# One head's K in four loads, the merge's gates two chunks ahead, and the output weights' splits shared out anew

## The chip, the cores and the metric

The kernel runs on one core of a Trainium2 chip. The metric is the device time of one execution in microseconds (us). The engines are named as in the profile: PE (TensorE, matrix multiplications), DVE (VectorE), ACT (ScalarE), POOL (GpSimd) and SP (SyncE, which here issues every DMA, in program order).

## The reference

One layer of a diffusion backbone, for 1024 latent tokens and 128 context tokens, D = 1024, 8 heads in each of two branches:

```python
h = layernorm(x) * (1 + scale) + shift            # adaLN, scale/shift/gate from the condition
qa, ka, va, za, qr, kr, vr, zr = split(h @ w_in)
oa = (softmax(q1 k1^T / 8) - lam * softmax(q2 k2^T / 8)) @ v   # keys: cached context + latent tokens
oa = (rmsnorm(oa) * subln_g * (1 - lam_init) * silu(za)) @ w_pa
orr = retention(qr, kr, vr, forward) + retention(backward)     # chunkwise recurrence
orr = (layernorm(orr) * ret_gn_g * silu(zr)) @ w_pr
ga, gr = split(sigmoid(h @ w_gate + b_gate))
m = ga * oa + gr * orr
y = layernorm(2**0.25 * x + gate * (m @ w_out)) * ln_g + ln_b
```

Context tokens read only context; latent tokens read both. Outputs are y and the context's keys, values and retention states.

## The kernel before, in words

All 1152 tokens (1024 latent, 128 context) are held as columns. Every float32 operand of a matmul is split into a high part and a low part of the type float32r, and each product is three matmuls (high by high, high by low, low by high). `hi_of` makes a high part on ACT, `lo_of` the low part on DVE ("v") or POOL ("p").

A dense job (`Job`) multiplies one block of 128 output columns' weights with all tokens, in NC = 3 chunks of CW = 384 tokens, 24 matmuls a chunk, into a PSUM bank called `dn`, of which there are two. Its `pre(c)` runs ahead of a chunk, its `evac(c, ps)` empties the bank. `dense` loads and splits the weights one job ahead (tiles `raw`, `whi`, `wlo`).

The whole program is emitted in one order. A small planner (`Sched`) keeps a modelled time for PE, ACT, DVE and POOL, lets several Python generators take turns at it, and so fixes the order of the instructions on every engine. `sch.later` puts off a piece of work to a modelled time; `sch.guard(tag, bufs)` makes such pieces run at once, so that a buffer can be taken again. DMAs cost the planner nothing: they go into SP's queue at the place where they are called, and SP runs them in that order, each waiting for its buffer and its data.

The stages, by the time in the profile:

- up to about 580 us: adaLN, projections, retention (`phase_h`, `phase_a`). Each head's rotated K is stored as high and low parts in `Kd`, 2 x 1280 columns for each of 128 partitions.
- about 590 to 1316 us: attention (`phase_b`). `softmax_stream` goes through `seq`, 8 heads h of 5 steps c; a step is two tiles of 128 queries (c = 4 one tile, the context's). At the start of a step it asks for the next step's Q (`load_q`, four DMAs), at c = 1 for the next head's K (`load_k`). Scores go to the one PSUM buffer `S`; DVE takes the maximum `nm`, ACT the exponentials `E`. `pv_stream` transposes E, splits it and multiplies with V (`load_v`). Between these matmuls the planner puts dense jobs: gates (`g_job`), the retention branch's silu gate (`zr_job`), the attention branch's (`z_job`). These two end in `gate_out`, which uses the tiles `tz`, `goh`, `gol` (two buffers each) and stores `goh` and `gol` to `ORd` or `OAd`. The gates go to `Gd` as tanh(u/2).
- about 1380 to 1486 us, the first merge pass: 8 jobs `pr_job(j)` multiply the retention branch (tiles `X`, two of them in K's buffers) with `w_pr`. The evacuation multiplies by the gate, read back from `Gd` into a tile `gt`, and stores the product in `Td`. `merge_in(kind, j, c)` issues the gate's load: for a chunk's successor, at the end of its evacuation. Meanwhile the attention branch comes back from `OAd` into `Y`, and `ada_gate` computes the adaLN gate on DVE.
- about 1486 to 1590 us, the second: `pa_job(j)` does the same for the attention branch, adds the product read back from `Td` into a `tz` tile, and writes the sum's high and low parts to `X`. In its last job the weights `w_out` arrive in eight pieces (`w_out_load(n)`) and the first four are split (`w_out_split(n)`) into the place of `Y`; the other four are split right after it. Pieces 0 to 3 hold the left half of the output columns, two row blocks each; 4 to 7 the right half.
- to the end: `out_stream`, the output product (PSUM tile `e`, 24 matmuls of 512 columns for a part) and the last LayerNorm. Its parts begin with the left halves of tiles 0 and 1, then their right halves.

## Time and profile before

| | |
|---|---|
| median of 3 runs | 1690.24 us (1687.55 to 1691.09) |
| the profiled execution | 1692.03 us, of which the span from first to last instruction is 1690.2 |
| granted TensorE clock, mean | 0.994 |
| PE busy | 1657.3 us, 98% of the span, 10515 matmuls |
| DVE, ACT, POOL busy | 853.6, 606.1, 784.4 us |
| DMA | 237.36 MB, mean 140 GB/s |

In a row of grouped or single instructions stand the start and the length in us, the engine, the line of the kernel, the operation, the tile written and the tiles read, the shape, and in brackets how long the engine stood idle before and what ended that. Many operations go through helpers, so that line 149 is every matmul, 156 every ACT operation, 164 and 173 DVE's, 185 and 189 POOL's, 203 every DMA: the tiles' names tell them apart. A row of stretches has the window, its length, then for PE, PEld, DVE, ACT and POOL the busy time with the number of instructions, then the granted clock, the DMA engines' busy share and GB/s. A row of the chain has start, length and what the chain ran through. A matmul's length in these rows overlaps the next one's, so paces are read from start to start.

### The profile page before, as it was taken

To read this page: it belongs to the slowest core of one execution; us is meant where nothing else is said; L and a number is where in the kernel's file an instruction comes from. 1 tells how busy PE (TensorE), PEld (TensorE's weight loads), DVE (VectorE), ACT (ScalarE), POOL (GpSimd) and SP (SyncE) were. 2 spreads that over 40 slices of the span, in tenths; PEclk is the share of its full clock that TensorE was granted. 3 is DMA by queue.
4 is the path that set the end of the run, shared out by engine and by line. 5 is a ranking of instruction groups with operands and counts; after the bars stand their busy time and mean duration, and the time that the engine had idled before them with its cause. 6 is when DMAs were issued, how large, how long until landed. Compare 5 with 4: busy or idle time off the path is not lost.

```text
span 1690.2 us, 27057 instructions
## 1 busy us (share of the span) xinstructions
PE 1657.3 (98%) x10515; PEld 1610.2 (95%) x10515; DVE 853.6 (51%) x1679; ACT 606.1 (36%) x1136; POOL 784.4 (46%) x546
## 2 busy tenths in 40 slices
PE   7999999999999999999999999999999999999998
PEld 4799999999999999999999999999999999999886
DVE  7736407314605536656565666566656033134666
ACT  5532222221221245455455555545555220012200
POOL 2246227334725657654757475757655321112200
PEclk9999999999999999999999999999999999999999
DMA  8254303421321383534434343525252577854532
GB/s 332 94 149 127 123 27 114 128 93 45 104 102 44 125 267 111 189 106 133 139 116 146 113 155 110 162 92 168 74 160 87 208 263 262 264 180 131 159 125 87
DMA packets 135697, 237.36 MB, mean 140 GB/s; under 512 B 15801, under 2 KB 103313, under 8 KB 134545
## 3 DMA queue, kind: packets, MB, share of 16 engines
q1 hardware_dynamic: 135568, 235.63, 43.3%
q8 instruction: 83, 1.36, 0.3%
q14 instruction: 46, 0.37, 0.1%
HBM read 161.08 MB, written 74.49 MB: 139 GB/s over the span
## 4 chain that ended last, share of the span: by engine, by line
PE 89%; DVE 3%; issue 2%; ACT 2%; DMA 1%; POOL 1%; SPq 0%; DVEq 0%; POOLq 0%; ACTq 0%
PE dn L149 59%; PE S L149 8%; PE o L149 6%; PE e L149 6%; PE a L149 5%; PE tp L153 5%; PE tp L149 1%; ACT E L156 1%; DMA xt<-in_x 1%; DMA ORd<-goh 0%; DVE eps L173 0%; DVE r L173 0%; DVE E L173 0%; ACT whi L156 0%; DVE nm L1097 0%
## 5 line engine op out<-in xcount | busy, mean ns | idle before, releaser
L149 PE MATMUL dn<-Y,whi 128*128 128x384 f32 x3200 | 829.7, 340 | 3.3 <-DVE rt L164 2.2
L149 PEld LDWEIGHTS dn<-Y,whi 128*128 128x128 f32 x3200 | 567.4, 189 | 4.9 <-DVE rt L164 2.5
L149 PE MATMUL dn<-Y,wlo 128*128 128x384 f32 x1600 | 535.6, 336 | 0.0
L185 POOL TENSOR_TENSOR wlo<-raw,whi 128x1024 fp32r<-128x1024 f32 x85 | 204.7, 2412 | 412.5 <-ACT whi L156 403.1
L149 PEld LDWEIGHTS dn<-Y,wlo 128*128 128x128 f32 x1600 | 300.5, 188 | 1.4 <-issue 0.9
L1097 DVE TENSOR_REDUCE nm<-S 128x1 f32<-128x1152 f32 x144 | 178.1, 1237 | 174.2 <-PE S L149 173.9
L189 POOL TENSOR_SCALAR E<-E,r 128x640 f32<-128x640 f32 x64 | 143.6, 2243 | 127.5 <-DVE r L173 87.0
L156 ACT ACTIVATE E<-S,nm 128x1152 f32<-128x1152 f32 x144 | 162.3, 1127 | 79.4 <-DVE nm L1097 74.5
L149 PE MATMUL dn<-whi,Y 128*128 128x256 f32 x864 | 158.9, 284 | 2.4 <-ACT vr L156 1.9
L149 PEld LDWEIGHTS dn<-whi,Y 128*128 128x128 f32 x864 | 135.4, 191 | 2.8 <-ACT vr L156 2.1
L149 PE MATMUL o<-wTh,V 128*128 128x256 f32 x576 | 133.5, 290 | 0.0
L156 ACT ACTIVATE wTh<-tp 128x512 fp32r<-128x512 f32 (+1 forms) x168 | 88.6, 543 | 112.9 <-PE tp L153 109.2
L156 ACT ACTIVATE whi<-raw 128x1024 fp32r<-128x1024 f32 x88 | 92.2, 1054 | 91.2 <-PE dn L149 85.0
L149 PE MATMUL dn<-wlo,Y 128*128 128x256 f32 x432 | 122.1, 283 | 0.0
L164 DVE TENSOR_TENSOR wTl<-tp,wTh 128x512 fp32r<-128x512 f32 (+1 forms) x168 | 99.6, 612 | 24.0 <-ACT wTh L156 24.0
L185 POOL TENSOR_TENSOR E<-E 128x640 f32<-128x640 f32 x64 | 100.4, 1569 | 5.3
L149 PE MATMUL S<-K,QH 128*128 128x384 f32 (+1 forms) x400 | 94.4, 339 | 6.2 <-ACT E L156 6.2
L149 PEld LDWEIGHTS o<-wTh,V 128*128 128x128 f32 x576 | 99.4, 188 | 0.2
L149 PE MATMUL S<-K,QL 128*128 128x384 f32 (+1 forms) x400 | 92.6, 335 | 0.0
L173 DVE SCALAR_TENSOR_TENSOR gt<-gt,dn 128x384 f32<-128x384 f32 x48 | 26.6, 554 | 120.2 <-DMA gt<-Gd 59.6
L153 PE MATMUL tp<-ident,E 128*128 128x128 f32 x584 | 86.8, 272 | 0.0
L169 DVE TENSOR_SCALAR KD<-tp,kdec 128x256 f32<-128x256 f32 (+1 forms) x48 | 16.0, 407 | 138.1 <-PE tp L153 138.1
(203 smaller groups left out, 2476.5 us busy)
## 6 DMA issues: line engine op xcount, KB each, us to landing
K<-Kd SPq DMA_DIRECT2D x8, 1280.0 KB, 8.3
Gd<-gt SPq DMA_DIRECT2D x48, 192.0 KB, 2.5
V<-Vd SPq DMA_DIRECT2D x24, 384.0 KB, 4.9
gt<-Gd SPq DMA_DIRECT2D x48, 192.0 KB, 2.5
Y<-OAd SPq DMA_DIRECT2D x16, 576.0 KB, 3.9
raw<-in_w_gate SPq DMA_DIRECT2D x16, 512.0 KB, 3.6
QH<-Qh SPq DMA_DIRECT2D x64, 128.0 KB, 3.0
QL<-Ql SPq DMA_DIRECT2D x64, 128.0 KB, 2.8
```

Source lines behind the costliest of these rows:

```text
L149: nc.tensor.matmul(out, lhsT=lhsT, rhs=rhs, start=start, stop=stop)
L153: nc.tensor.transpose(out, in_, ident)
L156: nc.scalar.activation(out, in_, func, **kw)
L164: nc.vector.tensor_tensor(out, a, b, op=op)
L169: nc.vector.tensor_scalar(out, a, s1, s2, op0=op0, **kw)
L173: nc.vector.scalar_tensor_tensor(out, a, s, b, op0=op0, op1=op1, **kw)
L185: nc.gpsimd.tensor_tensor(out, a, b, op=op)
L189: nc.gpsimd.tensor_scalar(out, a, s1, None, op0=op0)
L1097: nc.vector.tensor_reduce(nm[:, m:m + 1], ps[:, :nb, :kw], axis=AX.XY, op=ALU.max, negate=True)
```

## The change

Three edits, each of DMAs or of the engine that does a split; the matmuls and their order in the program are left as they are.

1. `load_k` loads only the first 320 of K's 1280 columns at c = 1 (both halves, 320 KB); a new `load_k_part` loads the next three parts at c = 2, 3 and 4. For the first head all four are issued at the stage's start.
2. In the first merge pass the gate is asked for two chunks ahead. Every second chunk's gate takes a `tz` buffer in place of a `gt` buffer; pending work of `gate_out` on those buffers is made to run before. At the pass's end the second pass's first two chunks are asked for a chunk earlier.
3. The low part of output weight piece n is computed on POOL for n = 2, 5, 7 and on DVE for the others; before, it was POOL for even n and DVE for odd n.

```diff
@@ -1016,12 +1016,18 @@
 
             t = kx.tile([P, 2, 1280], F32R, tag="K", name="K", bufs=2)
             if h < NH:
-                dma(t.bitcast(F32), Kd[h])
                 Kt[h] = t
+                load_k_part(h, 0)
             else:
                 X[h - NH] = t[:, :, :NT]
                 if ("gate_out", h - NH, False) in done:
                     load_x(h - NH)
+
+        def load_k_part(h, q):
+
+            if h < NH:
+                ks = slice(q * 320, (q + 1) * 320)
+                dma(Kt[h][:, :, ks].bitcast(F32), Kd[h, :, :, ks])
 
         vseq = [(h, g) for h in range(NH) for g in range(3)]
 
@@ -1060,6 +1066,8 @@
                     load_q(*seq[si + 1])
                 if c == 1:
                     load_k(h + 1)
+                elif c:
+                    load_k_part(h + 1, c - 1)
                 K = Kt[h]
                 QH, QL = Qt[h, c]
                 lat = c < 4
@@ -1289,14 +1297,20 @@
 
         def merge_in(kind, j, c):
 
-            if c == NC:
-                j, c = j + 1, 0
+
+            if c >= NC:
+                j, c = j + 1, c - NC
             if j == KT:
                 kind, j = kind + 1, 0
             if kind == 2 or (kind, j, c) in D_:
                 return
             cs = slice(c * CW, (c + 1) * CW)
-            g = pz.tile([P, CW], F32, tag="gt", name="gt", bufs=2)
+            if kind == 0 and (NC * j + c) % 2:
+                sch.guard("silu", 1)
+                sch.guard("tz", 1)
+                g = pz.tile([P, CW], F32, tag="tz", name="gt", bufs=2)
+            else:
+                g = pz.tile([P, CW], F32, tag="gt", name="gt", bufs=2)
             dma(g, Gd[8 + j if kind == 0 else j, :, cs])
             if kind == 0:
                 D_[kind, j, c] = g
@@ -1308,6 +1322,8 @@
         def pr_job(j):
             def pre(c):
                 merge_in(0, j, c)
+                if (j, c) == (0, 0):
+                    merge_in(0, 0, 1)
                 if c:
                     dma(Y[:, c - 1, j, :].bitcast(F32), OAd[c - 1, j])
 
@@ -1315,7 +1331,7 @@
                 t = D_[0, j, c]
                 f = v_stt(t, t, 1.0, ps, ALU.add, ALU.mult)
                 dma(Td[j, :, c * CW:(c + 1) * CW], t)
-                merge_in(0, j, c + 1)
+                merge_in(0, j, c + 2)
                 return f
 
             return Job("W", [I["w_pr"][j]], lambda k: X[k], evac, pre=pre,
@@ -1335,7 +1351,7 @@
             hs = Y[:, 0, 2 * k2:2 * k2 + 2, g * 512:(g + 1) * 512]
             ls = Y[:, 1, 2 * k2:2 * k2 + 2, g * 512:(g + 1) * 512]
             f = hi_of(hs, r3)
-            lo_of("v" if n % 2 else "p", ls, r3, hs, f)
+            lo_of("p" if n in (2, 5, 7) else "v", ls, r3, hs, f)
 
         def pa_job(j):
             def pre(c):
@@ -1405,6 +1421,8 @@
         psum_pool(es, "S", 1)
         psum_pool(es, "o", 1)
         load_k(0)
+        for q in range(1, 4):
+            load_k_part(0, q)
         load_q(0, 0)
         sch.run([softmax_stream(), pv_stream(), stream], lambda: "B" in done)
         es.close()
```

## The prediction

> **What bounds the kernel now.** I read the page first, then the chain that ended last, then stretches, then the single instructions beside each hole of TensorE (PE).

> ```profile
> span 1690.2 us, 27057 instructions
> PE 1657.3 (98%) x10515; PEld 1610.2 (95%) x10515; DVE 853.6 (51%) x1679; ACT 606.1 (36%) x1136; POOL 784.4 (46%) x546
> ...
> 717.00:730.00 13.00, 10.50 (x59) 10.06 (x58) 6.14 (x11) 5.84 (x12) 6.40 (x5) 0.87 0.33 112
> 730.00:1310.00 580.00, 576.23 (x3772) 570.81 (x3771) 349.13 (x581) 311.44 (x602) 354.65 (x221) 1.00 0.40 127
> 1380.00:1486.00 106.00, 102.94 (x583) 102.22 (x583) 31.17 (x54) 8.75 (x9) 20.63 (x9) 0.98 0.78 263
> ...
> 1582.00:1590.00 8.00, 6.87 (x30) 5.15 (x29) 7.25 (x5) 2.87 (x5) 4.94 (x2) 1.00 0.62 194
> ...
> 1440.61 122.19 PE dn L149 x705
> ```

> PE is the bound at 98%. In the stretches the first figure after the length is PE's busy time, the third last the granted clock. What can be won lies where PE is idle or its clock is down: 13 us in the second head's attention (2.50 idle, clock 0.87), the first merge pass at 1380 to 1486 (3.06 idle, clock 0.98), and the start of the output stage (1.13 idle). The chain's long piece gives the price of an undisturbed 384-wide matmul: 122.19 / 705 = 0.173 us.

> The hole in the second head, followed back:

> ```profile
> 710.11 0.60 SPq L203 DMA_DIRECT2D K<-Kd  x1
> ...
> 710.81 8.18 DMA ORd<-goh
> ...
> 716.18 0.49 ACT L156 ACTIVATE tz<-dn 128x384 f32<-128x384 f32 x1 [3.29 <-PE dn L149]
> ...
> 719.01 0.49 ACT L156 ACTIVATE goh<-dn 128x384 f32<-128x384 f32 x1 [2.34 <-DMA ORd<-goh]
> ...
> 717.92 0.34 PE L149 MATMUL dn<-Y,wlo 128*128 128x384 f32 x1
> 720.76 0.79 PE L149 MATMUL S<-K,QH 128*128 128x384 f32 x3 [2.50 <-ACT E L156]
> ...
> 722.09 4.18 PE dn L149 x15
> ...
> DMA to landing us min/median/max: 1.8/2.0/7.7
> ```

> The next head's K is one transfer of 1280 KB. A 192 KB store of `goh` issued 0.7 us behind it needs 8.18 us; stores and loads of `goh` take 2.0 as a median (last row). ScalarE (ACT) wants that buffer and stands 2.34 us with the next exponential queued behind it; PE's scores wait for the exponential. From start to start, less one step, PE loses 720.76 - 717.92 - 0.17 = 2.67 us. Then it runs slow: 15 matmuls in 4.18 us where 15 x 0.173 = 2.60 belong, 1.58 more.

> The first merge pass:

> ```profile
> 1406.34 0.34 PE L149 MATMUL dn<-X,wlo 128*128 128x384 f32 x1
> 1407.72 0.62 PE L149 MATMUL dn<-K,whi 128*128 128x384 f32 x2 [1.05 <-DVE gt L173]
> ...
> 1428.20 0.42 SPq L203 DMA_DIRECT2D gt<-Gd  x1
> ...
> 1434.41 0.56 DVE L173 SCALAR_TENSOR_TENSOR gt<-gt,dn 128x384 f32<-128x384 f32 x1 [5.46 <-issue]
> ...
> 1432.67 0.34 PE L149 MATMUL dn<-X,wlo 128*128 128x384 f32 x1
> 1435.02 0.62 PE L149 MATMUL dn<-K,whi 128*128 128x384 f32 x2 [2.01 <-DVE gt L173]
> ...
> 1435.02 5.49 PE dn L149 x21
> ...
> DMA to landing us min/median/max: 1.8/2.5/6.1
> ```

> A chunk is 24 matmuls, 24 x 0.173 = 4.2 us. Its gate is asked for only when the chunk before has been evacuated, and two banks of `dn` let PE run one chunk ahead. Before the second hole VectorE (DVE) starts 6.2 us after the gate's issue, which agrees with the slowest landing of 6.1 (last row, this tile's transfers). PE loses 1407.72 - 1406.34 - 0.17 = 1.21 and 1435.02 - 1432.67 - 0.17 = 2.18 us, and after the second 5.49 - 21 x 0.173 = 1.85 us more at low clock.

> **The change part by part.** The sum is made against the profiled execution, 1692.03 us (span 1690.2), 1.8 above the median of 1690.24 and 4.5 above the fastest run, so some of these holes probably vary from run to run.

> *The clock.* The slow stretches follow holes of 2.18 and 2.67 us; after the hole of 1.21 the pace is normal. I take a hole of over 2 us to cost some 1.6 to 1.9 us extra. [...]

> *K in four parts.* One 1280 KB transfer becomes four of 320 KB, issued at steps 1 to 4 of the head before. Per head three more issues on SP's queue; each K issue took 0.60 us, so the stores and loads behind it there (`goh`, `gol`, gates, weights, V) come 0.6 us later, three times, and in the second head the `goh` store still stands behind part 0. ACT is ready for that buffer at 716.18 + 0.49 = 716.67, 5.9 us after the store's issue. A quarter of K delays the store by about a quarter of what K did: 2.0 + (8.18 - 2.0) / 4 = 3.5 us. The wait is gone. Late next is ACT's own row: in the trace the exponential's result freed PE 1.75 us after `goh` began (719.01 to 720.76); from 716.6 that is 718.3, against PE free at 718.1, so 0.2 us stay and no slow stretch. Gain 2.67 + 1.58 - 0.2 = 4.0 us. Ends: 0 (the store is late for another reason) and 4.25.

> Part 3 has the shortest lead. It stands behind the Q loads of the last step:

> ```profile
> K<-Kd SPq DMA_DIRECT2D x8, 1280.0 KB, 8.3
> ...
> V<-Vd SPq DMA_DIRECT2D x24, 384.0 KB, 4.9
> ...
> 679.61 1.22 SPq L203 DMA_DIRECT2D QL<-Ql  x2
> ...
> 688.62 0.68 PE L149 MATMUL S<-K,QH 128*128 128x384 f32 x3
> ...
> 1037.07 1.22 SPq L203 DMA_DIRECT2D QL<-Ql  x2
> ...
> 1043.23 0.77 PE L149 MATMUL S<-K,QH 128*128 128x384 f32 x3
> ```

> Only the third score matmul reads the last columns: 688.97 - 680.83 = 8.1 us at the first head's end and about 5.3 at the fifth's, the shortest of the seven. The part is nearest to V's 384 KB at 4.9 us, so I take nothing; ends 0 and what K's 8.3 would give (third rival).

> *The first head's K.* Three more issues stand ahead of its Q loads, 1.8 us; the bytes ahead of them are the same. PE ran without a hole there and I take 0. Ends 0 and 1.8.

> *Gates two chunks ahead.* Odd chunks use the two `tz` buffers, even ones the two `gt`. Each gate is now issued 8.4 us before its product is due, over the slowest landing of 6.1; its buffer's store went out two chunks before. Both waits and the slow stretch go: 1.21 + 2.18 + 1.85 = 5.2 us. What ends DVE's idle time next is PE itself. No instruction is added but the gate asked for early at the start, and the guards find nothing pending, since the last head's gating is over by then. The loads for the second pass's first two chunks also move up by a chunk on SP's queue, and one `tz` load there waits on SP for the store of the chunk just done, with the next gate and a weight load behind it: about 2.5 us (a gate's median landing, the nearest row), two chunks ahead of need, so nothing. Ends 0 and 5.2.

> *Output weights.* Before, the low parts alternate: even ones on GpSimd (POOL), odd ones on DVE. After, 0, 1 and 3 are DVE's and 2 is POOL's; of the last four, 4 and 6 are DVE's, 5 and 7 POOL's.

> ```profile
> 1580.10 2.94 ACT L156 ACTIVATE Y<-raw 128x1024 fp32r<-128x1024 f32 x3
> ...
> 1581.22 5.72 POOL L185 TENSOR_TENSOR Y<-raw,Y 128x1024 fp32r<-128x1024 f32 x2 [18.41 <-ACT Y L156]
> ...
> 1582.12 2.57 DVE L164 TENSOR_TENSOR Y<-raw,Y 128x1024 fp32r<-128x1024 f32 x1 [1.34 <-ACT Y L156]
> 1584.61 3.40 DVE L164 TENSOR_TENSOR Y<-wo,Y 128x1024 fp32r<-128x1024 f32 x1
> ...
> 1582.45 0.40 PE L149 MATMUL e<-Y,K 128*128 128x512 f32 x1
> 1583.66 1.43 PE L149 MATMUL e<-Y,K 128*128 128x512 f32 x5 [0.82 <-POOL Y L185]
> 1584.93 1.75 PE L149 MATMUL e<-Y,X 128*128 128x512 f32 x7
> 1586.99 2.79 PE L149 MATMUL e<-Y,X 128*128 128x512 f32 x11 [0.31 <-POOL Y L185]
> ...
> 1590.98 4.24 PE L149 MATMUL e<-Y,X 128*128 128x512 f32 x18
> 1595.06 1.52 PE L149 MATMUL e<-Y,K 128*128 128x512 f32 x6
> ```

> Eighteen matmuls from 1590.98 to 1595.06 are 0.227 each. PE loses 1583.66 - 1582.45 - 0.23 = 0.98, then 1584.93 - 1583.66 - 5 x 0.227 = 0.14, then 1586.99 - 1584.93 - 7 x 0.227 = 0.47: 1.6 us. The durations only fit if DVE and POOL take turns: DVE's second ends at 1588.01, 1.07 after POOL's pair ends at 1586.94. So DVE needs about 1.07 alone, POOL 2.3. Now ACT has the first high part at 1581.1; DVE gives split 0 at 1582.3 and 1 at 1583.4, both ahead of PE (1582.7 and 1584.0). POOL then does 2 until 1585.7, PE wants it at 1582.45 + 13 x 0.227 = 1585.4: 0.3 to 0.4 us stay. Split 3 follows at 1586.8, wanted at 1587.1. Gain 1.2 us. Splits 4 to 7 are wanted from 1593.7 on and nothing about them is tight. Ends -0.5 (DVE delayed by the last evacuation) and 1.6.

> Sum: 4.0 + 5.2 + 1.2 = 10.4; 1692.03 - 10.4 = 1681.6 us.

> **The rivals.**
> 1. *Another wait takes K's place.* V (384 KB) and weights (512 KB) still share the DMA engines, and ACT's order is unchanged, so `goh` or something else can hold the exponentials for the 4.0 us. For it: the stretch 730 to 1310 has 3.77 us idle over five more K loads, so small holes come with K or without. Against it: the 8.18 us stands behind K alone. Time 1685.6.
> 2. *Gates remain late.* DMA is busy 0.78 at 263 GB/s in this pass with the same bytes; if throughput and not lead is short, more lead only postpones the wait. Against it: the median landing is 2.5 us. Time 1681.6 + 5.2 = 1686.8.
> 3. *Slower: the last K part lands late at each head's end.* If it takes K's whole 8.3 us, each of seven ends loses 0.2 to 3.0 us, 1.6 as their middle, 11 in all, and some three holes over 2 us cost 1.7 each of clock: 1681.6 + 16 = 1698. It decides (over 1693.6) from a loss of 12 us, a landing of about 7.8 us. Against it: V's 4.9 at more bytes. [...]
> 4. *Nothing moves.* All holes are replaced by equal ones: 1692.

> **How the numbers follow.** The forecast 0.62, the rivals 0.18, 0.09, 0.05 and 0.06. About 0.2% (3.4 us) is what a measurement tells from no change, so faster means under 1686.9 and slower over 1693.6. Faster: 0.62 + 0.18 and half of the second rival, which lies on the bound, 0.84; same 0.05 + 0.06 = 0.11; slower 0.05. The forecast's own range is 1679.8 (the median's 1.8 under the profiled run, taken off again) to 1683.4 (the first K's 1.8). The range reaches to the first two rivals, 1.2 us beyond, and at the low end to small holes gone as well: 1679.0 to 1688.0.

> **What would show it.** Right: no wait of ACT on `ORd<-goh` in the second head, a clock of 1.00 there; no wait on `gt<-Gd` that PE feels from 1380 on, that pass some 5 us shorter; one hole of under half a us at the first output tile. Wrong: score matmuls waiting for `K<-Kd` at a head's start, ACT still waiting for a store with PE behind it, or DVE waiting for gates.

## The result and the profile after

The changed kernel takes 1680.93 us (median of 4 runs, 1679.78 to 1681.77) against 1690.02 (4 runs); the ratio is 0.9948, with a 95% interval of 0.9931 to 0.9965. The profiled execution went from 1692.03 to 1680.88 us, 11.15 us less; between the medians it is 9.1 us. 1681.6 had been forecast.

Both programs run the same 10515 matmuls in the same order, so the two traces can be laid over each other matmul by matmul, and the lead of the new one read off at any point. Where it grew:

| stretch, in the time of before | gained, us | forecast |
|---|---|---|
| start to 705 us | -0.2 | 0 |
| second head, 705 to 732 | 4.0 | 4.0 |
| rest of the attention, to 1310 | 1.0 | 0 |
| first merge pass | 5.2 | 5.2 |
| second merge pass | 0.0 | 0 |
| output's start | 1.1 | 1.2 |
| sum | 11.1 | 10.4 |

The stretches of the changed kernel that answer to those shown of before (start and end, length, then the busy time of PE, PEld, DVE, ACT, POOL, then the granted clock, the DMA engines' share, GB/s):

```profile
717.00:730.00 13.00, 12.95 (x87) 12.51 (x86) 7.43 (x12) 8.74 (x17) 10.26 (x8) 1.00 0.35 106
730.00:1310.00 580.00, 576.93 (x3783) 571.65 (x3782) 350.11 (x582) 311.00 (x601) 353.15 (x219) 1.00 0.43 129
1375.00:1476.00 101.00, 101.00 (x585) 100.92 (x584) 31.49 (x54) 8.76 (x9) 23.04 (x9) 1.00 0.85 282
1571.00:1580.00 9.00, 8.74 (x41) 7.16 (x40) 7.32 (x7) 5.03 (x7) 2.67 (x1) 1.00 0.54 177
```

PE has no idle time left in the first merge pass, 0.05 us in the second head's stretch and 0.26 at the output's start, and the clock is full in all four. In the rest of the attention 3.07 us of 580 are left, of 3.77 before. DMA is busier in the merge pass than before, 0.85 against 0.78: nearly the same bytes (28.5 MB against 27.9, by the rates) in 5 us less.

The second head, as single instructions of SP, ACT and PE:

```profile
710.34 0.60 SPq L203 DMA_DIRECT2D K<-Kd  x1
711.05 0.55 SPq L203 DMA_DIRECT2D ORd<-goh  x1
...
716.41 0.49 ACT L156 ACTIVATE tz<-dn 128x384 f32<-128x384 f32 x1 [3.29 <-PE dn L149]
716.79 0.49 ACT L156 ACTIVATE goh<-dn 128x384 f32<-128x384 f32 x1
...
718.15 0.34 PE L149 MATMUL dn<-Y,wlo 128*128 128x384 f32 x1
718.53 0.80 PE L149 MATMUL S<-K,QH 128*128 128x384 f32 x3
```

The store of `goh` still goes out 0.7 us behind K's load, but now behind 320 KB. ACT takes the buffer without a wait, at 716.79, and PE's scores start 718.53 - 718.15 - 0.17 = 0.21 us late, where 0.2 had been worked out.

Who waited for whom in the merge pass, first before, then after (total us, times, longest):

```profile
DVE gt L173 <- DMA gt<-Gd: 55.2, 17, 9.0
DVE gt L173 <- issue: 15.0, 5, 5.5
DVE gt L173 <- PE dn L149: 8.1, 2, 4.9
```

```profile
DVE gt L173 <- PE dn L149: 59.8, 20, 3.6
...
DVE gt L173 <- DMA gt<-Gd: 9.1, 1, 9.1
```

DVE still idles for some 70 us (68.9 in these rows, 78.3 before), but what ends its idle time is now mostly PE's product and no longer the gate's transfer. The one wait on a gate that is left is the pass's first chunk.

The output's start:

```profile
1570.11 2.94 ACT L156 ACTIVATE Y<-raw 128x1024 fp32r<-128x1024 f32 x3
...
1571.18 2.36 DVE L164 TENSOR_TENSOR Y<-raw,Y 128x1024 fp32r<-128x1024 f32 x2 [0.39 <-ACT Y L156]
...
1573.13 2.67 POOL L185 TENSOR_TENSOR Y<-raw,Y 128x1024 fp32r<-128x1024 f32 x1 [20.31 <-ACT Y L156]
...
1574.03 2.85 DVE L164 TENSOR_TENSOR Y<-wo,Y 128x1024 fp32r<-128x1024 f32 x1 [0.48 <-ACT Y L156]
...
1572.46 1.55 PE L149 MATMUL e<-Y,K 128*128 128x512 f32 x6
1573.85 1.75 PE L149 MATMUL e<-Y,X 128*128 128x512 f32 x7
1575.85 1.43 PE L149 MATMUL e<-Y,X 128*128 128x512 f32 x5 [0.26 <-POOL Y L185]
```

Two low parts from DVE are there before PE asks; POOL's ends at 1575.80, and PE loses 1575.85 - 1573.85 - 7 x 0.227 = 0.41 us on it.

### The profile page after: what moved, and what is told of

Same layout as the page of the kernel before. It is cut to its first block, busy times and chain, and to the rows that moved or that the text cites. A ratio compares the mean times of both kernels' runs of the same rounds, so it can differ in the third digit from the quotient of the medians.

```text
span 1679.1 us, 27069 instructions
## 1 busy us (share of the span) xinstructions
PE 1653.6 (98%) x10515; PEld 1606.8 (96%) x10515; DVE 851.9 (51%) x1680; ACT 606.1 (36%) x1136; POOL 784.6 (47%) x545
## 4 chain that ended last, share of the span: by engine, by line
PE 91%; DVE 3%; ACT 2%; DMA 2%; POOL 1%; issue 0%; SPq 0%; DVEq 0%; ACTq 0%; POOLq 0%
PE dn L149 61%; PE S L149 8%; PE o L149 6%; PE e L149 6%; PE tp L153 5%; PE a L149 4%; PE tp L149 1%; DMA xt<-in_x 1%; ACT E L156 0%; SPq L203 0%; ACT Y L156 0%; ACT hf L156 0%; DMA RE<-in_ret_const 0%; DMA Vd<-vh 0%; DVE eps L173 0%
## 5 line engine op out<-in xcount | busy, mean ns | idle before, releaser
L149 PE MATMUL dn<-Y,whi 128*128 128x384 f32 x3200 | 830.2, 340 | 3.3 <-DVE rt L164 2.2
L149 PEld LDWEIGHTS dn<-Y,whi 128*128 128x128 f32 x3200 | 567.4, 189 | 4.8 <-DVE rt L164 2.5
L149 PE MATMUL dn<-Y,wlo 128*128 128x384 f32 x1600 | 535.8, 336 | 0.0
L185 POOL TENSOR_TENSOR wlo<-raw,whi 128x1024 fp32r<-128x1024 f32 x85 | 206.9, 2437 | 406.9 <-ACT whi L156 388.1
L149 PEld LDWEIGHTS dn<-Y,wlo 128*128 128x128 f32 x1600 | 300.6, 188 | 1.4 <-issue 1.3
L156 ACT ACTIVATE E<-S,nm 128x1152 f32<-128x1152 f32 x144 | 162.4, 1128 | 81.2 <-DVE nm L1105 75.3
L149 PE MATMUL dn<-whi,Y 128*128 128x256 f32 x864 | 157.4, 283 | 2.0 <-ACT vr L156 1.2
L149 PEld LDWEIGHTS dn<-whi,Y 128*128 128x128 f32 x864 | 134.1, 189 | 2.4 <-ACT vr L156 1.4
L149 PE MATMUL o<-wTh,V 128*128 128x256 f32 x576 | 133.5, 290 | 0.0
L156 ACT ACTIVATE wTh<-tp 128x512 fp32r<-128x512 f32 (+1 forms) x168 | 88.6, 543 | 112.1 <-PE tp L153 108.4
L156 ACT ACTIVATE whi<-raw 128x1024 fp32r<-128x1024 f32 x88 | 92.2, 1055 | 90.7 <-PE dn L149 83.6
L149 PE MATMUL dn<-wlo,Y 128*128 128x256 f32 x432 | 121.4, 281 | 0.0
L164 DVE TENSOR_TENSOR wTl<-tp,wTh 128x512 fp32r<-128x512 f32 (+1 forms) x168 | 99.4, 612 | 23.5 <-ACT wTh L156 23.5
L185 POOL TENSOR_TENSOR E<-E 128x640 f32<-128x640 f32 x64 | 100.4, 1569 | 5.3
L149 PEld LDWEIGHTS o<-wTh,V 128*128 128x128 f32 x576 | 99.4, 188 | 0.1
L149 PE MATMUL S<-K,QH 128*128 128x384 f32 (+1 forms) x400 | 94.6, 340 | 4.0 <-ACT E L156 4.0
L149 PE MATMUL S<-K,QL 128*128 128x384 f32 (+1 forms) x400 | 92.6, 335 | 0.0
L173 DVE SCALAR_TENSOR_TENSOR gt<-gt,dn 128x384 f32<-128x384 f32 x48 | 26.6, 554 | 114.6 <-PE dn L149 101.2
## 6 DMA issues: line engine op xcount, KB each, us to landing
V<-Vd SPq DMA_DIRECT2D x24, 384.0 KB, 3.8
```

Of the source, the lines that this page charges most:

```text
L149: nc.tensor.matmul(out, lhsT=lhsT, rhs=rhs, start=start, stop=stop)
L156: nc.scalar.activation(out, in_, func, **kw)
L164: nc.vector.tensor_tensor(out, a, b, op=op)
L173: nc.vector.scalar_tensor_tensor(out, a, s, b, op0=op0, op1=op1, **kw)
L185: nc.gpsimd.tensor_tensor(out, a, b, op=op)
```

## The experiments

The theory was that each edit removes holes of its own, by the steps of the prediction. The first four kernels take the edits apart; the last one of them asks what it is about K in parts that helps.

**K in four parts alone**, the other two edits left out:

```diff
-                dma(t.bitcast(F32), Kd[h])
                 Kt[h] = t
+                load_k_part(h, 0)
...
                 if c == 1:
                     load_k(h + 1)
+                elif c:
+                    load_k_part(h + 1, c - 1)
```

> K in four parts alone, the rest as before. Theory (the three edits each remove their own holes, independently): the hole at 718 us in the second head and the slow matmuls after it go, some 4 us, so about 1686 to 1688 us; the two holes of the first merge pass and the one at the output's start stay as they were (about 5.2 and 1.6 us). Rival (the holes are one chain: with K's hole gone another wait takes its place, or the merge's holes move with it): under 1.5 us gained, or holes at other places.

Measured: 1686.21 us (11 runs, 1684.43 to 1687.3) against 1689.53, ratio 0.9981 (0.9973 to 0.999). The hole at 718 us is gone, and the trace gains 4.0 us there, as that of the changed kernel. The merge pass keeps holes, though this time other ones, each ended by DVE:

```profile
1420.96 0.62 PE L149 MATMUL dn<-K,whi 128*128 128x384 f32 x2 [0.54 <-DVE gt L173]
1430.18 0.62 PE L149 MATMUL dn<-K,whi 128*128 128x384 f32 x2 [0.62 <-DVE gt L173]
1434.98 0.28 PE L153 MATMUL tp<-ident,gc 128*16 128x128 f32 x1 [0.86 <-DVE gc L164]
```

So what the pass loses depends on how its transfers meet in a run: 5.2 us in the trace of before, 3.4 here, by laying this trace over the same matmuls.

**Gates two chunks ahead alone** (the diff of `merge_in` and `pr_job`, K and the splits as before).

> Gates two chunks ahead alone. Theory: the first merge pass runs without a hole and takes some 5 us less, about 1685 to 1687 us; the hole behind the 1280 KB load of K in the second head stays at 2 to 3 us with slow matmuls after it. Rival (the merge's waits come from DMA throughput, not from the lead of the gates): holes stay in the pass, at other chunks, and under 2 us are gained.

Measured: 1686.44 us (median of 11 runs, 1682.98 to 1689.17), ratio 0.998 (0.9969 to 0.9991). A twelfth run took 2724.2 us and is not in these numbers; no trace of it was kept, and its cause is open. A stretch of the merge pass and the hole in the second head:

```profile
1375.00:1481.00 106.00, 106.00 (x614) 105.92 (x613) 33.74 (x58) 10.87 (x12) 21.80 (x9) 1.00 0.81 273
```

```profile
720.68 0.84 PE L149 MATMUL S<-K,QH 128*128 128x384 f32 x3 [2.94 <-ACT E L156]
```

The pass runs without a hole with DMA 0.81 busy, so throughput was not short, and K's hole stays, longer than before (2.94 us idle).

**The splits alone.**

```diff
-            lo_of("v" if n % 2 else "p", ls, r3, hs, f)
+            lo_of("p" if n in (2, 5, 7) else "v", ls, r3, hs, f)
```

> Output weights' splits shared as after, the rest as before. Theory: 1.1 to 1.2 us at the output's start and nothing else, about 1689 us, hardly to be told from no change by the time, but seen in the trace as one hole of 0.4 us in place of about 1.6. Rival (DVE becomes late in the output stage): holes of PE later in that stage, no gain.

Measured: 1688.6 us, ratio 0.9993 (0.9983 to 1.0003): by time nothing that can be told. The trace has the one hole that was expected and gains 1.1 us at the output's start, no more later and no less:

```profile
1583.99 2.81 PE L149 MATMUL e<-Y,X 128*128 128x512 f32 x11 [0.26 <-POOL Y L185]
```

Elsewhere this trace differs from that of before, though nothing was changed there: behind the whole K of the second head it loses 1.2 us and not 4.0, since ACT stood 1.1 us for a store of `goh` in this trace, against 2.34 before, and the hole of 1.30 us brought no slow matmuls.

The three ratios add up to 0.46% (0.19, 0.20 and 0.07), against 0.52% (0.35 to 0.69) for all together: they add, as far as these intervals tell.

**All four parts of K at once**, on the changed kernel:

```diff
                 if c == 1:
                     load_k(h + 1)
-                elif c:
-                    load_k_part(h + 1, c - 1)
+                    for q in range(1, 4):
+                        load_k_part(h + 1, q)
```

> The changed kernel, but the four parts of K are all issued together at step 1. Theory (bytes that stand ahead on the DMA queue delay the store of goh): the store lands about 8 us after its issue again, PE loses 2 to 3 us at 718 us plus slow matmuls, 3 to 4.5 us more than the changed kernel, about 1685 us. Rival (it is the size of K's pieces, 10 KB rows against 1.25 KB ones, that lets the store pass): the store lands in 4 us or less, no hole, the changed kernel's time, about 1681 us.

Measured: 1687.93 us (12 runs, 1684.99 to 1693.4), ratio 0.9996. SP's queue, the chain and PE:

```profile
711.15 2.56 SPq L203 DMA_DIRECT2D K<-Kd  x4
...
713.81 6.42 DMA ORd<-goh
...
722.00 0.79 PE L149 MATMUL S<-K,QH 128*128 128x384 f32 x3 [2.71 <-ACT E L156]
```

The hole is back, 2.71 us idle behind a store of 6.42 us, so in this trace pieces with short rows did not let the store pass; what stands ahead of the store counts. The loss was underestimated: 7 us over the changed kernel instead of 3 to 4.5. Four issues hold SP for 2.56 us where one took 0.60, so the store leaves 2.7 us behind K's first issue and not 0.7, besides landing slowly; and in this trace holes of about 1.1 and 1.6 us follow the K loads of two later heads. The two were not separated by a run. An estimate from these rows: in the changed kernel ACT wants the buffer 5.7 us after the store's issue (716.79 - 711.05), so the landing of 6.42 us alone would make it 0.7 us late, and the later issue adds 2.0.

The next four ask for place, lead and buffers.

**K as one load, at step 3**, the rest as changed:

```diff
-                if c == 1:
+                if c == 3:
                     load_k(h + 1)
```

(with `load_k` as before the change).

> The changed kernel with K again as one load of 1280 KB, but issued at step 3 of the head before instead of step 1. Theory (any 1280 KB ahead of the stores on the queue holds ACT up wherever a buffer of goh or a gate is wanted soon): the hole at 718 us goes, but some other head gets one of 1 to 3 us behind its K load; 1683 to 1687 us, and the runs scatter by several us. Rival (it was one unlucky meeting at step 1, any other place will do): no hole behind a K load, about 1681 us, as the changed kernel.

Measured: 1680.02 us (4 runs, 1678.82 to 1682.13), ratio 0.9943 (0.9929 to 0.9956): the rival was right. In the second head the store now follows Q, and no landing of `goh` that the trace holds took more than 5.0 us:

```profile
708.48 1.22 SPq L203 DMA_DIRECT2D QL<-Ql  x2
709.79 0.55 SPq L203 DMA_DIRECT2D ORd<-goh  x1
```

```profile
DMA to landing us min/median/max: 1.8/1.9/5.0
```

A whole K of 1280 KB, asked for early enough, did no harm here, where no store with a tight deadline stands behind it. Of the change's two features, a spread and a smaller piece at step 1, neither was needed; only step 1 had to be kept clear.

**K as one load, at step 4** (the same with 4), to price a late last part.

> The changed kernel with K as one load of 1280 KB at step 4, the last, which prices a late last part. Theory: the load needs about 8 us and the lead to the first score matmuls of the next head is 5 to 8 us, so scores wait for K at most of the seven head ends, 0.2 to 3.5 us each, about 11 us with 2 to 3 spells of slow matmuls: 1690 to 1698 us. Rival (the load at this place lands in 5 us, or PE has other work there): under 3 us lost, 1681 to 1684 us.

Measured: 1686.5 us (10 runs, 1682.34 to 1690.21), 6.5 over the load at step 3. PE at two heads' ends, and K's landings:

```profile
778.87 1.30 PE L149 MATMUL S<-K,QH 128*128 128x384 f32 x3 [4.86 <-issue]
...
1047.73 0.77 PE L149 MATMUL S<-K,QH 128*128 128x384 f32 x3 [2.47 <-DMA K<-Kd]
```

```profile
DMA to landing us min/median/max: 4.8/6.6/10.4
```

Of the seven ends only two have such a hole, the second and the fifth head's. The price by the end was right or too low, the number of ends was not. The row holds every load into K's buffers, and its 10.4 is the first head's. The two landings at head ends that the trace holds are 6.6 and 6.7 us, at ends without a hole; the two scores that were late began 10.0 and 7.6 us after their K's issue (768.85 and 1040.15). For the first of them the profile names no releaser; that it is K is inferred, since the load at step 3 has no such hole.

**Gates two ahead in two buffers**, on the changed kernel:

```diff
-            if kind == 0 and (NC * j + c) % 2:
...
-                g = pz.tile([P, CW], F32, tag="tz", name="gt", bufs=2)
-            else:
-                g = pz.tile([P, CW], F32, tag="gt", name="gt", bufs=2)
+            g = pz.tile([P, CW], F32, tag="gt", name="gt", bufs=2)
```

> The changed kernel with the gates two chunks ahead but in the two gt buffers alone, so that each gate's load stands on SP until the product of the chunk just done is stored from the same buffer. Theory (the lead is what counts): SP waits 2 to 2.5 us for each of 24 stores, the gates still have some 5 us of lead against a median landing of 2.9, so the pass has at most one hole of about 1 us: 1681 to 1683 us. Rival (the two more buffers are what counts): the loads of Y and of the weights behind the wait come late, gates come late again, holes of over 2 us in the pass: 1685 us or more.

Measured: 1725.27 us, ratio 1.0209 (1.0195 to 1.0223), 44 us over the changed kernel. SP's queue in the pass, and PE at the start of the second:

```profile
SPq L203 <- DMA Td<-gt: 102.0, 24, 5.5
```

```profile
1519.26 0.69 PE L149 MATMUL dn<-Y,whi 128*128 128x384 f32 x1 [6.25 <-DMA Y<-OAd]
```

SP stands 4.25 us for each of the 24 stores (102.0 / 24) and not 2 to 2.5. Every store but the first has a load of `Y` (576 KB) or of weights (512 KB) less than 2 us ahead of it on the queue. Of the landings that the trace holds, those are 3.6 to 5.9 us; that of the first store is 1.9. The whole queue waits with it: gates, weights, and `Y`, which the second pass then finds missing. The rival was right, by more than it said.

**Four buffers, one chunk ahead**: the other half of that edit.

```diff
-                if (j, c) == (0, 0):
-                    merge_in(0, 0, 1)
...
-                merge_in(0, j, c + 2)
+                merge_in(0, j, c + 1)
```

> The changed kernel with the gates' four buffers, but each gate asked for only one chunk ahead, as before the change. Theory (a gate's lead over its landing decides, the buffers only keep SP from waiting): the pass has its holes again, 1 to 2 us each at two or three chunks and perhaps slow matmuls, 3 to 6 us in all: 1684 to 1687 us. Rival (the waits came from the buffers): no holes, about 1681 us.

Measured: 1684.46 us (12 runs, 1680.58 to 1687.51), 4.8 over the changed kernel on the same chip (1679.68). The pass has holes again:

```profile
1428.91 0.62 PE L149 MATMUL dn<-K,whi 128*128 128x384 f32 x2 [1.67 <-DVE gt L173]
1433.72 0.28 PE L153 MATMUL tp<-ident,gc 128*16 128x128 f32 x1 [0.87 <-DVE gc L164]
```

The lead does it, and the two more buffers are what makes this lead possible without SP waiting for a store: with two buffers it stands 102.0 us for `Td<-gt`, in the changed kernel's pass not once.

Three kernels try whether more is to be had.

**Piece 2 on DVE too** (`n in (5, 7)` for POOL).

> The changed kernel with the low part of piece 2 on DVE as well, so that POOL has no split before the output starts. Theory (what is left of the output's hole, 0.42 us, is POOL's start on piece 2 while DVE holds the shared turn, and its 2.3 us): the hole goes, under 0.1 us stays, since DVE then gives a low part every 1.07 us from 1571 us on and ACT a high part every 0.98; about 0.4 us, not to be told from the changed kernel by the time (1680.5). Rival (DVE falls behind with four): a hole of 0.5 us or more moves to piece 3 or to the last evacuation.

Measured: 1679.65 us (5 runs), ratio 0.9941 (0.9928 to 0.9953). DVE and PE at the output's start:

```profile
1571.31 3.50 DVE L164 TENSOR_TENSOR Y<-raw,Y 128x1024 fp32r<-128x1024 f32 x3 [0.39 <-ACT Y L156]
...
1573.97 4.25 PE L149 MATMUL e<-Y,X 128*128 128x512 f32 x18
```

Three parts in 3.50 us, 1.17 each, with no split of POOL beside them, and PE goes through the rest of its part in one piece. The trace gains 0.6 us there over the changed kernel's, somewhat more than the 0.4 that was left; the time does not show it.

**K at step 2**, as one load.

> The changed kernel with K as one load at step 2. Theory now (a 1280 KB load hurts only where a store of goh stands right behind it on the queue with ACT wanting the buffer within some 8 us, as in the second head's step 1): no hole of over 1 us behind a K load, 1680 to 1682 us. Rival (step 3 was a lucky place, bursts hurt in general): a hole of 1 to 3 us in some head, 1683 us or more.

Measured: 1680.62 us (4 runs, 1679.63 to 1680.81), ratio 0.9941: no hole over 1 us behind a K load, as the narrowed theory has it.

**K at step 3 and piece 2 on DVE together**, and **the changed kernel again** beside it.

> The changed kernel with K as one load at step 3 and all of the first four low parts on DVE, the two forms that did no worse alone. Theory: nothing is left of K's holes, the first merge pass has none, the output starts without one: about 1679.5 us, 1 us under the changed kernel if the single load gives back the issues on SP and the small holes of the attention. Rival (both are within the scatter): 1680 to 1681 us, as the changed kernel.

> The changed kernel itself, beside the others on one chip: 1680 to 1682 us by either theory; its scatter over the runs about 2 us against 5 to 8 of the kernel before.

Measured: 1679.04 us (6 runs, 1678.28 to 1681.96; ratio 0.9935, 0.9915 to 0.9954) and 1679.68 us (6 runs, 1679.04 to 1682.34; ratio 0.9937, 0.9916 to 0.9958). The combination beats the kernel before; that it beats the changed one is not shown.

## Why the prediction was right

Point by point, by its own steps:

- *K in four parts, 4.0 us*: 4.0 in the trace, and the same at the same place in every trace that has no whole K or burst at step 1. The mechanism is shown by moving K in both directions. The size is one draw: the traces with a whole K or a burst there lose 4.0 (before), 4.5 (gates alone), 1.2 (the splits alone) and 4.2 us (burst), and alone the edit took 3.3 us off the median. What the prediction did not see is that the spread is not needed for it.
- *Part 3's lead*: the parts land in 4.0 us as a median, against the 4.9 of V that was taken, and no score waits for one:

```profile
K<-Kd SPq DMA_DIRECT2D x32, 320.0 KB, 4.0
```

 One load of 1280 KB at step 3 and four of 320 KB give 1680.0 and 1680.9 us: a larger transfer neither helps nor hurts here, as far as these two times tell.
- *The first head's K, 0 with an end of 1.8*: four issues take 3.52 us, so the Q loads go out 2.9 us later, more than that end. It stayed hidden: the first scores start at 604.72, 0.13 us later than before, with no hole.

```profile
590.68 3.52 SPq L203 DMA_DIRECT2D K<-Kd  x4
...
604.72 0.68 PE L149 MATMUL S<-K,QH 128*128 128x384 f32 x3
```

- *Gates, 5.2 us*: 5.2 in the trace. In the time it is less clear: alone 0.20% (0.09 to 0.31), some 3.4 us, and 4.8 us when the lead is taken away again. The pass lost 5.2, 3.4, 6.0 and 4.0 us in the four traces with gates one ahead (before, K alone, the splits alone, four buffers), so that a single profile lay near their middle was luck.
- *Output weights, 1.2 us, 0.3 to 0.4 left*: 1.1, with 0.41 left. That DVE and POOL take turns was read from before, and the output's rows agree: a split of DVE takes 2.85 us beside POOL's (1574.03 in the changed kernel) and 1.22 us with none of POOL's beside it (1574.72, piece 2 on DVE); with POOL's split taken away the hole went.
- *The rest of the attention, 0*: this term was missed, at 1.0 us. Between 1138 and 1194 us the trace gains 1.3; the last K load is issued there at 1149 us in the kernel before, and the kernels with K in parts, or at step 2, 3 or 4, all gain 1.3 to 1.5 us at that place, while those that load K whole or in a burst at step 1 do not. So a second of the eight K loads cost something, less than the first. Here it is another small store that stands behind K: `RSd`, which is read back at once into `rb`. The reading load goes out 3.7 us after the store's issue in the kernel before and 1.8 in the changed one, and POOL waits for it, first before, then after:

```profile
1159.82 1.01 POOL L185 TENSOR_TENSOR o_sb<-o_sb,rb 128x384 f32<-128x384 f32 x1 [4.14 <-DMA rb<-RSd]
```

```profile
1154.68 1.01 POOL L185 TENSOR_TENSOR o_sb<-o_sb,rb 128x384 f32<-128x384 f32 x1 [2.48 <-DMA rb<-RSd]
```

 In the chain that ended last this leads over POOL and ACT to PE's scores.
- *The clock*: the size of a slow spell, 1.6 to 1.9 us, was right at 1.7; that it takes a hole of over 2 us was not; see below.
- *Which run*: the working was done against one execution, 1.8 us above the median, and between medians the gain is 9.1 us where 10.4 was added up. The time after came out at 1680.9 all the same, because the holes of that execution were subtracted from that execution's time. The runs of before, on all chips, lie between 1684.71 and 1697.40 (71 of them), those of the changed kernel between 1679.04 and 1682.34 (10). What the change takes away is also a good part of what made the runs differ.

Of the rivals, the first (another wait) and the second (throughput) did not happen. The third, a late last part, happened with the load at step 4, which cost 6.5 us; a quarter of K, at 4.0 us as a median, held up no score.

## What to carry to other kernels

When a wait ends on a small store or load that took several times its median (here 8.18 us against 2.0), look for what was issued just ahead of it on the same queue; moving the large transfer to a place where nothing urgent follows can do as well as cutting it up (1680.02 and 1680.93 us), and issuing the pieces together cured nothing here (1687.93). A buffer's load wants a lead over its slowest landing, not over its median: of the gates' loads of before the slowest took 6.1 us and the median 2.5, and one chunk of lead left holes of 1.21 and 2.18 us, two chunks none. On a queue that waits in order that lead needed more buffers (here four in place of two): without them the queue itself stood still, 4.25 us for each of 24 stores, at a far higher price (44 us). A hole of one profile is one draw: count what the same place loses in several traces before giving it a size.

## What the runs showed of the hardware

A slow spell of PE does not need a hole of 2 us. Two kernels (K at step 3 with piece 2 on DVE, then K at step 3) have the same hole of 1.2 us at the same place, the context's short step of a head; first its stretch, then the matmul that ends it:

```profile
1119.00:1128.00 9.00, 7.76 (x37) 7.41 (x38) 5.90 (x9) 1.80 (x6) 6.52 (x5) 0.81 0.41 135
...
1120.95 0.33 PE L149 MATMUL S<-K,QH 128*128 128x128 f32 x1 [1.24 <-ACT E L156]
```

```profile
1120.00:1129.00 9.00, 7.77 (x49) 7.42 (x49) 6.55 (x11) 3.22 (x9) 6.46 (x5) 1.00 0.42 139
...
1121.86 0.33 PE L149 MATMUL S<-K,QH 128*128 128x128 f32 x1 [1.23 <-ACT E L156]
```

One is followed by a spell at low clock, 9 us at 0.81, so 1.7 us lost; the other by none, 9 us at 1.00. Nor did a longer hole always bring one at once: behind the 2.47 us of K at step 4 (1047.73) the 384-wide matmuls start 0.18 to 0.22 us apart up to 1049.84, where its rows end, and not 0.32 as in the spell of the first of the two (1122.41 to 1122.73). In the trace of before, cut at the places where the clock changes, three spells are 3.41 us at a granted clock of 0.50, 1.7 us lost in each:

```profile
94.18:97.59 3.41, 3.41 (x18) 3.41 (x17) 2.71 (x8) 2.54 (x8) 1.00 (x1) 0.50 0.49 108
722.24:725.65 3.41, 3.41 (x13) 3.40 (x12) 2.44 (x3) 1.72 (x3) 0.34 (x1) 0.50 0.00 0
1435.62:1439.03 3.41, 3.41 (x13) 3.41 (x12) 2.81 (x6) 0.00 (x0) 0.00 (x0) 0.50 0.81 269
```

The hole of 1.23 us stands at the context's short step of the first and of the sixth head in these two traces too. It ends at 686.21 and 1126.67 us in before and at 686.43 and 1123.20 in the changed kernel, 1.52, 1.66, 0.27 and 0.13 us behind such a place, a whole number of 3.4133 us from the clock's changes, and none of the four brought a spell (clock 1.00). The first of the two holes above ended 2.53 us behind one (1120.95 - 1118.42), and its spell began at the next, 0.88 us later:

```profile
1118.42:1121.83 3.41, 2.17 (x15) 1.86 (x15) 2.34 (x4) 0.46 (x2) 3.41 (x3) 1.00 0.23 94
1121.83:1125.24 3.41, 3.41 (x12) 3.41 (x11) 2.20 (x3) 1.34 (x4) 3.33 (x3) 0.50 0.51 149
```

Of these five, the one that ended late brought a spell and the four that ended earlier none. They are too few for a rule: why one hole brings a spell and the next does not is not shown.
